# Attention heads scaled ahead of weight pieces, and the spread reciprocals read ahead of a weight load

## The chip, the cores and the metric

The kernel runs on one core of a Trainium2 chip. A core has a matrix engine (TensorE, written PE in the profile, with its weight loads as PEld), a vector engine (VectorE, DVE), an activation engine (ScalarE, ACT), a general engine (GpSimd, POOL), and a sync engine (SyncE, SP) that here issues nearly all transfers between the chip's main memory (HBM) and the on-chip memory. Sixteen DMA engines carry the transfers out. Each engine takes its instructions in the order in which they were written, and waits where an instruction needs what another engine or a transfer has not finished. The metric is the device time of one execution in microseconds (us); lower is better. The number given is the median of several runs.

## The reference

One decoder layer for 256 tokens of width 1024, all in float32: two token mixers side by side (attention with eight heads of 64, and a causal pooling over four window lengths), gated and added, then a feed-forward part with a short causal convolution. Cut to what matters here:

```python
h = rmsnorm(x, norm_mix_g)
q, k, v, u_pool, gate_logits = split(h @ w_in)
attn = moba_attention(rotary(rmsnorm(q)), rotary(rmsnorm(k)), v)  # SEQ = one block: causal softmax attention
pooled = multiscale_pool_mixer(u_pool, w_pool, pool_scale)
gates = sigmoid(gate_logits + b_gate)                              # (B, S, 2, D)
mixed = gates[:, :, 0] * (attn @ w_branch_attn) + gates[:, :, 1] * (pooled @ w_branch_pool)
x = x + mixed @ w_out
up = causal_depthwise_conv(rmsnorm(x, norm_ffn_g) @ w_up, conv_w, conv_b)
gate, val = split(up)
return x + (silu(gate) * val) @ w_down
```

The sequence of 256 is exactly one block of the block-sparse attention, so no earlier block can be chosen and plain causal attention remains.

## The kernel before

**Split operands.** Every large product is made of three matmuls on a shortened float32 type: with each operand split into a high part and the rest, it adds high x high, high x rest and rest x high (helper `mm3`, lines 103 to 105). For a weight tile of 128 x 2048 the high part is an ACT copy (`hi_...`, line 91) and the rest is a DVE subtraction (`lo_...`, line 95), each made in two pieces of 128 x 1024. Raw tiles go round in four buffers (`raw_...`). The list `order` gives the sequence of the weights: q, k, v, p (pooling input), g (gate logits), `bp` and `ba` (the two branch weights, two tiles each), `o` (four tiles), then `up` and `dn`. A piece is made wherever the program calls `ahead()`, which writes one high piece on ACT and one rest piece on DVE; when the last rest piece of a tile is written, `loads()` (line 135 issues) starts the load of the tile four places on. So the place of `ahead()` calls sets at which point in ACT's and DVE's queues the pieces stand, and through the buffers when SP can load.

**Stages.** Projections q, k, v; the pooling inputs; sixteen tiles of gate logits (`ps_g`), during which the scores and the softmax of the attention are done on DVE and ACT; then eight tiles of the pooling branch (`ps_bp`, loop over `j` from 0 to 7, called branch bp here), with the product of the softmax weights and the values (`values`, tile `ps_o`, line 625) written behind tile `j = 4` (`VALUES = 4`); then eight tiles of the attention branch (`ps_ba`), the output projection (`ps_out`), and the feed-forward part (`ps_up`, `ps_d`). Four PSUM banks go round among the tiles of the branches, so tile n+4 needs the bank that DVE has emptied of tile n.

**The attention's last steps.** The softmax weights are turned by 32 x 32 blocks on DVE and through HBM (`spill`, `fill`; transfers `home_w`, then `y<-home_w`). The sums of the exponentials are inverted, written to HBM (`home_sums`), and read back so that each reciprocal stands beside its values (tile `RS`, two reads, line 613, in `fill_late`). While the second half of the softmax is under way, loads are held back (`paused`), and `fill_late` writes one held load, `ba`'s second tile, ahead of the two reads of `RS`. `rounded` multiplies the values in PSUM by `RS` (DVE, line 644, four instructions of 128 x 256) and writes the high part of `heads` (ACT, line 91, four); `rests` writes the rest part of `heads` (DVE, line 95, four). `heads` is the moving operand of every matmul of `ps_ba`.

**Around them in the loop of bp.** Each `j` has on DVE the product of the finished bank with its gate (line 733) and, for `j` below 6, a product of one gate with the spread inverse norm `R1` (line 735); on ACT a sigmoid of one gate (line 656); and pieces of weights where `ahead()` is called. In the loop of `ps_ba`, DVE multiplies the bank by a gate (line 754), POOL adds the pooling branch (line 755), ACT writes the high part `mh` and DVE the rest `ml` for the output projection.

Of the kernel before, what the change touches and what calls it, by code (L numbers as in the profile page):

```python
# [10 lines left out]
ALU = mybir.AluOpType  # L11
# [3 lines left out]
S = 256  # L15
NT = S // P
D = 1024
KD = D // P
# [38 lines left out]
VALUES = 4  # L57
# [13 lines left out]
def hybrid_layer_kernel(ctx: ExitStack, tc: tile.TileContext, xq_d, xtok_d, par_d, wkv_d, wpg_d,  # L71
                        wpool_d, wba_d, wbp_d, wout_d, wup_d, wdn_d, out_d):
    nc = tc.nc
# [12 lines left out]
    def bank(name):  # L86
        return mm.tile([P, 512], F32, tag="mm", name=name)


    def high(hi, src, scale=1.0):  # L90
        nc.scalar.activation(hi, src, AF.Copy, scale=scale)  # L91

    def low(lo, hi, src, scale=None):
        if scale is None:
            nc.vector.tensor_tensor(lo, src, hi.bitcast(F32), ALU.subtract)  # L95
        else:
            nc.vector.scalar_tensor_tensor(lo, src, scale, hi.bitcast(F32), ALU.mult, ALU.subtract)
# [25 lines left out]
    def load(parts=1):  # L123
        c = loaded[0]
        if c == len(order):
            return
        loaded[0] += 1
        name, src = order[c]
        n = src.shape[-1]
        if c in cut_loads:  # L130
            parts = 2
        raws[c] = raw_p.tile([P, CH], F32, tag="raw", name=f"raw_{name}{c}")
        for i in range(parts):
            sl = slice(i * n // parts, (i + 1) * n // parts)
            nc.sync.dma_start(out=raws[c][:, sl], in_=src[:, sl])
# [53 lines left out]
    def loads(most=None):  # L189

        while loaded[0] - RAWBUFS in split and order[loaded[0] - RAWBUFS][0] != "q" and loaded[0] < len(order):
            if paused[0] if most is None else most == 0:
                break
            load()
            most = most if most is None else most - 1
# [3 lines left out]
    def ahead(upto=0):  # L199

        next_high()
        next_low()
        if at[1] - sum(p[0] < used[0] for p in pieces) < upto:
            next_high()
            next_low()

    def chunk(name):
        c = used[0]
        used[0] += 1
        spent.update(i for i in range(c) if order[i][0] != "dn")  # L210
        assert order[c][0] == name and all(p[0] != c or name == "dn" and p[3] for p in pieces[at[1]:]), (name, order[c][0])
        return his[c], los[c]
# [222 lines left out]
    def tick():  # L435
        clock[0] += 1
        for fn, args in due.pop(clock[0], []):
            fn(*args)


    def feature_tile(w, c, name):
        hi, lo = w
        ps = bank(f"ps_{name}")
        for k in range(KD):
            sl = slice(k * 256 + c * P, k * 256 + (c + 1) * P)
            mm3(ps[:, 0:S], (hi[:, sl], lo[:, sl]), (xhi[:, k, :], xlo[:, k, :]), k == 0, k == KD - 1)
        return ps
# [32 lines left out]
    for b in range(2):  # L480
        w = chunk("p")
        for c in range(2):
            ps = feature_tile(w, c, f"u{b}{c}")
# [35 lines left out]
    def gate(n):  # L519
        return gates[:, n // 2, n % 2, :]  # L520
# [63 lines left out]
    def turn_weights(hp, y, sm):  # L584
        turn(y, sm)
        home = spill(y, f"w{hp}")
        if hp < 2:
            later(1, fill_weights, hp, home, sm)
            return
        late.append((hp, home, sm))  # L590
        if hp == H // 2 - 1:
            nc.vector.reciprocal(rsum[:, 0:2 * H], rsum[:, 0:2 * H])
            yr = const.tile([P, 32], F32, name="yr")
            nc.vector.transpose(yr, rsum)
            far = spill(yr, "sums")
            loads(1)
            later(1, fill_late, far)
# [3 lines left out]
    def fill_weights(hp, home, sm):  # L601
        fill(home, sm)
        soft[hp] = sm.rearrange("p (a n r) -> p a n r", a=4, r=32)

    def fill_late(far):

        for weights in late:
            fill_weights(*weights)
        loads(1)
        RS.append(act.tile([P, H // 2 * NT * P], F32, tag="qk", name="RS"))  # L610
        for j in range(2):
            src = far.rearrange("(a i) r -> a (i r)", a=4)[None, :, j * S:(j + 1) * S].to_broadcast([DH, 4, S])
            nc.sync.dma_start(out=RS[0][j * DH:(j + 1) * DH, :].rearrange("p (a c) -> p a c", a=4), in_=src)
        paused[0] = False
        loads()

    def values(hps):

        po = ps2.tile([P, 2, 512], F32, tag="ps2", name=f"ps_o{hps[0]}")
        for i, hp in enumerate(hps):  # L620
            for b in range(2):
                for j in range(2):
                    h = 2 * hp + j
                    out = po[j * DH:(j + 1) * DH, i, 0:S].rearrange("p (a t r) -> p a t r", a=4, r=32)
                    nc.tensor.matmul(out[:, :, b:2, :], vn[:, b, h * DH:(h + 1) * DH],
                                     soft[hp][:, :, 3 * j + 2 * b:3 * j + b + 2, :], start=b == 0, stop=b == 1)
        return po

    def weighed(hp):
        return RS[0].rearrange("p (a h t r) -> p h a t r", a=4, t=NT, r=32)[:, hp]  # L630

    def natural(hp):
        return weighed(hp).rearrange("p a t r -> p t a r")

    def tokens(head, hp):
        return head[:, hp, :].rearrange("p (t a r) -> p t a r", t=NT, r=32)

    def rounded(hps, po):
        if not heads:
            both = act.tile([P, 2, KA, S], F32R, tag="at", name="heads")  # L640
            heads.extend(both[:, i] for i in range(2))
        for i, hp in enumerate(hps):
            v = weighed(hp)
            nc.vector.tensor_tensor(v, po[:, i, 0:S].rearrange("p (a t r) -> p a t r", a=4, r=32), v, ALU.mult)
            high(tokens(heads[0], hp), natural(hp))

    def rests(hps):
        for hp in hps:
            low(tokens(heads[1], hp), tokens(heads[0], hp), natural(hp))
# [3 lines left out]
    def sigmoids(n):  # L653
        for _ in range(min(n, len(waiting))):
            f = waiting.pop(0)
            nc.scalar.activation(gate(f), gate(f), AF.Sigmoid, bias=par[:, C_BG + f:C_BG + f + 1])
# [20 lines left out]
    for n in range(2 * KD):  # L677
# [16 lines left out]
        ps = feature_tile(w, c, f"g{n}")  # L694
# [18 lines left out]
    def branch(src, oph, opl, j, w):  # L713
        hi, lo = w
        ps = bank(f"ps_b{src}{j}")
        for k in range(4):
            sl = slice(k * 512 + (j % 4) * P, k * 512 + (j % 4 + 1) * P)
            mm3(ps[:, 0:S], (hi[:, sl], lo[:, sl]), (oph[:, k, :], opl[:, k, :]), k == 0, k == 3)
        return ps

    for j in range(KD):
        if j % 4 == 0:
            w = chunk("bp")
        ps = branch("p", poolh, pooll, j, w)
        if j == VALUES:
            pos = [(hps, values(hps)) for hps in ((0, 1), (2, 3))]
        if j % 2 == 1:
            tick()
            ahead()
        if j in (0, 2, 4, 6):  # L730
            ahead()
        sigmoids(1)
        nc.vector.tensor_tensor(gate(KD + j), ps[:, 0:S], gate(KD + j), ALU.mult)
        if j < len(plain):
            nc.vector.tensor_tensor(gate(plain[j]), gate(plain[j]), R1, ALU.mult)
        if j == VALUES:
            for po in pos:
                rounded(*po)
        if j == VALUES + 1:
            for hps, _ in pos:  # L740
                rests(hps)
    mixer.close()
    tmp = ctx.enter_context(tc.tile_pool(name="ffn", bufs=2))
    mh = act.tile([P, KD, S], F32R, tag="qk", name="mh")
# [2 lines left out]
    for j in range(KD):  # L747
        if j % 4 == 0:
            w = chunk("ba")
        ps = branch("a", heads[0], heads[1], j, w)  # L750
# [47 lines left out]
    for b in range(4):  # L798
        w = chunk("o")
        ps = [bank(f"ps_out{b}{c}") for c in range(2)]  # L800
# [74 lines left out]
    def up_tile(w, c, i):  # L875
        ps = bank(f"ps_up{i}_{c}")
        tile_part(w, (hhi, hlo), c, ps, range(KD))
        return ps
# [15 lines left out]
    ps = [bank("ps_up1_0")]  # L894
# [6 lines left out]
    for i in range(1, KF):  # L901
        if i > 1:
            w = chunk("up")
            ps = [up_tile(w, 0, i)]
# [101 lines left out]
```

## Time and profile before

| what | value |
|---|---|
| median of three runs | 328.73 us (328.5, 328.73, 332.89) |
| the profiled execution's own time | 328.95 us |
| its span, first to last instruction | 327.2 us |
| PE busy in it | 322.8 us, 99% |
| DVE busy | 259.4 us, 79% |
| ACT busy | 201.6 us, 62% |
| POOL busy | 71.8 us, 22% |
| moved by DMA | 69.72 MB, mean 213 GB/s |
| granted TensorE clock | 1.000 |

The profile is one execution, taken by the hardware profiler. A row of the timeline gives the start in us from the start of the span, the duration, the engine, the line of the program, the operation, its tile and operands, how many such instructions follow each other, and in brackets how long the engine stood idle just before it and what ended that. Matmuls are pipelined: a row of 0.28 us is followed by the next start after about 0.113 us, so the distance of starts, and not the duration, tells what one costs. A row of DMA issues gives the size and the time from issue to landing.

### The profile page before, as it was taken

The page shows a single profiled execution, that of the slowest core. Times are in us where ns is not written, and L with a number is a line of the kernel's source. Part 1 is how long each engine was busy: PE and PEld are TensorE (multiplying, and loading weights), DVE is VectorE, ACT ScalarE, POOL GpSimd, SP SyncE. Part 2 cuts the span into 40 slices and gives each one's busy share as a digit, 9 for nine tenths or more (in the row PEclk, how much of TensorE's full clock was granted, in tenths as well). Part 3 has the DMA queues.
Part 4 walks back from the last instruction along what each step waited for, and adds up shares of the span by engine and source line. Part 5 has one row for each costly group of instructions (what it writes and reads, how often), then busy time and mean ns, then how long its engine had stood idle before and what let it go on. Part 6 is the DMA issues. An engine that isn't in the chain of part 4 may idle for free.

```text
span 327.2 us, 6768 instructions
## 1 busy us (share of the span) xinstructions
PE 322.8 (99%) x2708; PEld 316.1 (97%) x2708; DVE 259.4 (79%) x447; ACT 201.6 (62%) x329; POOL 71.8 (22%) x89
## 2 busy tenths in 40 slices
PE   8999999999999999999999999999999999999995
PEld 8888899999999999999999999999999999999995
DVE  4939989989988966879997978686868686868834
ACT  5767519665995657669675647474747474746520
POOL 1007690000000151230421221212121212121330
PEclk9999999999999999999999999999999999999999
DMA  7999799837799833735527456464645454643003
GB/s 258 422 412 240 218 385 284 299 138 268 270 255 312 372 128 131 241 146 179 207 97 290 179 207 221 165 214 175 214 172 217 170 213 173 221 165 130 0 2 128
DMA packets 16542, 69.72 MB, mean 213 GB/s; under 512 B 2176, under 2 KB 7040, under 8 KB 9856
## 3 DMA queue, kind: packets, MB, share of 16 engines
q1 hardware_dynamic: 16096, 69.17, 59.5%
q8 instruction: 21, 0.34, 0.4%
q10 hardware_dynamic: 416, 0.13, 0.2%
q14 instruction: 9, 0.07, 0.1%
HBM read 65.61 MB, written 3.69 MB: 212 GB/s over the span
## 4 chain that ended last, share of the span: by engine, by line
PE 99%; DVE 0%; issue 0%
PE ps_up L104 12%; PE ps_up L103 12%; PE ps_up L105 12%; PE ps_d L867 6%; PE ps_d L866 6%; PE ps_d L868 6%; PE ps_g L103 5%; PE ps_g L104 4%; PE ps_g L105 4%; PE ps_q L333 4%; PE ps_k L333 3%; PE ps_v L333 3%; PE ps_out L104 2%; PE ps_out L105 2%; PE ps_out L103 2%; PE ps_warm L248 1%
## 5 line engine op out<-in xcount | busy, mean ns | idle before, releaser
L105 PE MATMUL ps_up<-hhi,lo_up 128*128 128x256 f32 x352 | 97.3, 276 | 0.0
L104 PE MATMUL ps_up<-hlo,hi_up 128*128 128x256 f32 x352 | 97.3, 276 | 0.0
L103 PE MATMUL ps_up<-hhi,hi_up 128*128 128x256 f32 x352 | 97.3, 276 | 0.0
L104 PEld LDWEIGHTS ps_up<-hlo,hi_up 128*128 128x128 f32 x352 | 66.1, 188 | 0.0
L103 PEld LDWEIGHTS ps_up<-hhi,hi_up 128*128 128x128 f32 x352 | 66.1, 188 | 0.0
L105 PEld LDWEIGHTS ps_up<-hhi,lo_up 128*128 128x128 f32 x352 | 66.1, 188 | 0.0
L95 DVE TENSOR_TENSOR lo_up<-raw_up,hi_up 128x1024 fp32r<-128x1024 f32 x44 | 54.7, 1262 | 7.3 <-ACT hi_up L91 7.3
L867 PE MATMUL ps_d<-al,hi_dn 128*128 128x256 f32 x176 | 48.6, 276 | 0.0
L868 PE MATMUL ps_d<-ah,lo_dn 128*128 128x256 f32 x176 | 48.6, 276 | 0.0
L866 PE MATMUL ps_d<-ah,hi_dn 128*128 128x256 f32 x176 | 48.6, 276 | 0.0
L91 ACT ACTIVATE hi_up<-raw_up 128x1024 fp32r<-128x1024 f32 x44 | 44.1, 1046 | 0.0
L848 POOL TENSOR_TENSOR c_v<-c_g,c_v 128x256 f32<-128x256 f32 x22 | 16.2, 737 | 121.4 <-DVE c_v L831 121.4
L91 ACT ACTIVATE ah<-c_v 128x256 fp32r<-128x256 f32 x22 | 9.2, 418 | 45.6 <-POOL c_v L848 45.6
L103 PE MATMUL ps_g<-xhi,hi_g 128*128 128x256 f32 x128 | 35.6, 278 | 0.0
L105 PE MATMUL ps_g<-xhi,lo_g 128*128 128x256 f32 x128 | 35.4, 277 | 0.0
L104 PE MATMUL ps_g<-xlo,hi_g 128*128 128x256 f32 x128 | 35.4, 277 | 0.0
L866 PEld LDWEIGHTS ps_d<-ah,hi_dn 128*128 128x128 f32 x176 | 33.1, 188 | 0.0
L867 PEld LDWEIGHTS ps_d<-al,hi_dn 128*128 128x128 f32 x176 | 33.1, 188 | 0.0
L868 PEld LDWEIGHTS ps_d<-ah,lo_dn 128*128 128x128 f32 x176 | 33.0, 188 | 0.0
L95 DVE TENSOR_TENSOR lo_dn<-raw_dn,hi_dn 128x1024 fp32r<-128x1024 f32 x22 | 27.8, 1263 | 0.4 <-ACT hi_dn L91 0.4
L836 DVE TENSOR_TENSOR u_v<-ps_up,R 128x256 f32<-128x256 f32 x22 | 9.3, 422 | 20.9 <-PE ps_up L105 20.8
L873 POOL TENSOR_TENSOR al<-c_v,ah 128x256 fp32r<-128x256 f32 x22 | 22.0, 1002 | 11.6 <-ACT ah L91 11.6
(196 smaller groups left out, 781.5 us busy)
## 6 DMA issues: line engine op xcount, KB each, us to landing
raw_up<-in_wup SPq DMA_DIRECT2D x22, 1024.0 KB, 4.8
raw_g<-in_wpg SPq DMA_DIRECT2D x8, 1024.0 KB, 7.3
raw_dn<-in_wdn SPq DMA_DIRECT2D x8, 1024.0 KB, 4.9
raw_o<-in_wout SPq DMA_DIRECT2D x4, 1024.0 KB, 10.1
raw_dn<-in_wdn SPq DMA_DIRECT2D x6, 512.0 KB, 4.8
raw_v<-in_wkv SPq DMA_DIRECT2D x2, 1024.0 KB, 15.3
raw_p<-in_wpg SPq DMA_DIRECT2D x2, 1024.0 KB, 12.8
raw_bp<-in_wbp SPq DMA_DIRECT2D x2, 1024.0 KB, 5.5
```

The lines of the kernel that those rows point to most:

```text
L91: nc.scalar.activation(hi, src, AF.Copy, scale=scale)
L95: nc.vector.tensor_tensor(lo, src, hi.bitcast(F32), ALU.subtract)
L103: nc.tensor.matmul(out, sh, mh, start=start, stop=False, **kw)
L104: nc.tensor.matmul(out, sh, ml, start=False, stop=False, **kw)
L105: nc.tensor.matmul(out, sl, mh, start=False, stop=stop, **kw)
L333: nc.tensor.matmul(pt[t][:, c:c + wide], sx[:, k, t * P:(t + 1) * P], wx[:, sl], start=k == 0 and c == 0 and sx is xhi and wx is hi, stop= ...
L836: nc.vector.tensor_tensor(u, ps[:, 0:S], R2, ALU.mult)
L848: nc.gpsimd.tensor_tensor(uc[1], g[1], uc[1], ALU.mult)
L866: nc.tensor.matmul(o, hi[:, sl], acch[i], start=first, stop=False, skip_group_check=True)
L867: nc.tensor.matmul(o, hi[:, sl], accl[i], start=False, stop=False, skip_group_check=True)
L868: nc.tensor.matmul(o, lo[:, sl], acch[i], start=False, stop=i == KF - 1, skip_group_check=True)
L873: nc.gpsimd.tensor_tensor(accl[i], act_i, acch[i].bitcast(F32), ALU.subtract)
```

## The change

Two things are moved; no instruction is added or taken away, and all operands and sizes stay.

```diff
@@ fill_late @@
         for weights in late:
             fill_weights(*weights)
-        loads(1)
         RS.append(act.tile([P, H // 2 * NT * P], F32, tag="qk", name="RS"))
@@ loop over j of the pooling branch @@
         if j == VALUES:
             pos = [(hps, values(hps)) for hps in ((0, 1), (2, 3))]
+        if j in (VALUES, VALUES + 1):
+            nc.vector.tensor_tensor(gate(KD + j), ps[:, 0:S], gate(KD + j), ALU.mult)
+            for hps, po in pos:
+                rounded(hps, po) if j == VALUES else rests(hps)
         if j % 2 == 1:
             tick()
             ahead()
         if j in (0, 2, 4, 6):
             ahead()
         sigmoids(1)
-        nc.vector.tensor_tensor(gate(KD + j), ps[:, 0:S], gate(KD + j), ALU.mult)
+        if j not in (VALUES, VALUES + 1):
+            nc.vector.tensor_tensor(gate(KD + j), ps[:, 0:S], gate(KD + j), ALU.mult)
         if j < len(plain):
             nc.vector.tensor_tensor(gate(plain[j]), gate(plain[j]), R1, ALU.mult)
-        if j == VALUES:
-            for po in pos:
-                rounded(*po)
-        if j == VALUES + 1:
-            for hps, _ in pos:
-                rests(hps)
     mixer.close()
```

The held load is not lost: the call of `loads()` at the end of `fill_late`, behind the reads of `RS`, writes it. In the rows below a trailing number tells buffers of one name apart.

On SP, from the load of `ba`'s first tile to the first loads of `o` (`raw_ba` and `raw_o` are weight loads, `y` the turned softmax weights, `RS` the reciprocals), before:

```order
L135 DMA raw_ba_1132<-in_wba 128x2048
L304 DMA y_814<-home_w_1120 32x4x192 x4
L304 DMA y_814<-home_w_1125 32x4x192 x4
L135 DMA raw_ba_1185<-in_wba 128x2048
L613 DMA RS<-home_sums 64x4x256 x2
L135 DMA raw_o_1230<-in_wout 128x2048
```

and now:

```order
L135 DMA raw_ba_1132<-in_wba 128x2048
L304 DMA y_814<-home_w_1120 32x4x192 x4
L304 DMA y_814<-home_w_1125 32x4x192 x4
L612 DMA RS<-home_sums 64x4x256 x2
L135 DMA raw_ba_1188<-in_wba 128x2048
L135 DMA raw_o_1230<-in_wout 128x2048
```

The two reads of `RS` have moved ahead of the load of `ba`'s second tile.

On DVE, from the first rest piece of `ba`'s second tile to the emptying of bp's tile `j = 6` (rows of `xq<-ps_bp` empty a bank, rows of `xq<-xq,R` are the products with `R1`), before:

```order
L95 TENSOR_TENSOR lo_ba_1331<-raw_ba_1185,hi_ba_1330 128x1024
L733 TENSOR_TENSOR xq<-ps_bp_1373,xq 128x256
L735 TENSOR_TENSOR xq<-xq,R_169 128x256
L644 TENSOR_TENSOR RS<-ps_o_1386,RS 128x4x64 x2
L644 TENSOR_TENSOR RS<-ps_o_1395,RS 128x4x64 x2
L95 TENSOR_TENSOR lo_o_1405<-raw_o_1230,hi_o_1404 128x1024
L733 TENSOR_TENSOR xq<-ps_bp_1422,xq 128x256
L735 TENSOR_TENSOR xq<-xq,R_169 128x256
L95 TENSOR_TENSOR heads<-RS,heads 128x256 x4
L733 TENSOR_TENSOR xq<-ps_bp_1444,xq 128x256
```

and now:

```order
L727 TENSOR_TENSOR xq<-ps_bp_1373,xq 128x256
L643 TENSOR_TENSOR RS<-ps_o_1386,RS 128x4x64 x2
L643 TENSOR_TENSOR RS<-ps_o_1395,RS 128x4x64 x2
L95 TENSOR_TENSOR lo_ba_1331<-raw_ba_1188,hi_ba_1330 128x1024
L739 TENSOR_TENSOR xq<-xq,R_169 128x256
L727 TENSOR_TENSOR xq<-ps_bp_1422,xq 128x256
L95 TENSOR_TENSOR heads<-RS,heads 128x256 x4
L95 TENSOR_TENSOR lo_o_1415<-raw_o_1230,hi_o_1414 128x1024
L739 TENSOR_TENSOR xq<-xq,R_169 128x256
L737 TENSOR_TENSOR xq<-ps_bp_1444,xq 128x256
```

The second rest piece of `ba`'s second tile now stands behind the scaling of the values instead of ahead of it; the first rest piece of `o` stands behind the rest parts of `heads` and thereby still ahead of the emptying of `j = 6`, as the product with `R1` does.

On ACT, at the same place (`xq<-xq,par` is a sigmoid), before:

```order
L656 ACTIVATE xq<-xq,par 128x256 x2
L91 ACTIVATE hi_o_1404<-raw_o_1230 128x1024
L656 ACTIVATE xq<-xq,par 128x256
L91 ACTIVATE heads<-RS 128x256 x4
L91 ACTIVATE hi_o_1404<-raw_o_1230 128x1024
```

and now:

```order
L655 ACTIVATE xq<-xq,par 128x256 x2
L91 ACTIVATE heads<-RS 128x256 x4
L91 ACTIVATE hi_o_1414<-raw_o_1230 128x1024
L655 ACTIVATE xq<-xq,par 128x256
L91 ACTIVATE hi_o_1414<-raw_o_1230 128x1024
```

The high parts of `heads` have moved ahead of the first high piece of `o` and of one sigmoid. PE's and POOL's sequences are the same as before.

## The prediction

> **What bounds the kernel now.** I read the page's busy times first, then who PE waited for, then PE's rows at the place of the change, and last the queues of SP, ACT and DVE there.
>
> The first lines are from the page (busy time, and the chain that ended last by engine), the next three from the lists of waits of PE and of its weight loads (in total, times, longest, in us), and the last two the first projection's row and the end of the chain:
>
> ```profile
> PE 322.8 (99%) x2708; PEld 316.1 (97%) x2708; DVE 259.4 (79%) x447; ACT 201.6 (62%) x329; POOL 71.8 (22%) x89
> PE 99%; DVE 0%; issue 0%
> ...
> PE ps_warm L248 <- DVE ones L216: 1.1, 1, 1.1
> ...
> PEld ps_warm L248 <- DVE ones L216: 1.0, 1, 1.0
> PEld ps_bp L103 <- DVE xq L735: 0.2, 1, 0.2
> ...
> 5.05 1.20 PE L333 MATMUL ps_q<-hi_q,xhi 128*128 128x256 f32 x4
> ...
> 323.77 0.13 PE ps_d L868
> 323.92 0.42 DVE xq L930
> ```
>
> PE works without a pause from 5.05 us to the last product at 323.9. Its only wait is 1.1 us for the first constant, far ahead of the change, and its weight loads show one of 0.2 us in branch bp. The chain is PE for 99%. So what DVE, ACT and SP do sooner is worth nothing unless PE waits for it, and the rows leave at most 0.2 us of such waiting. The change can only lose, or do nothing.
>
> At the place of the change PE's rows read:
>
> ```profile
> 104.09 0.28 PE L105 MATMUL ps_bp<-poolh,lo_bp 128*128 128x256 f32 x1
> 104.30 1.52 PE L625 MATMUL ps_o<-sm,vn 128*64 128x256 f32 x16
> 105.65 1.47 PE L625 MATMUL ps_o<-y,vn 128*64 128x256 f32 x16
> 107.05 0.39 PE L103 MATMUL ps_bp<-poolh,hi_bp 128*128 128x256 f32 x1
> 107.28 0.28 PE L104 MATMUL ps_bp<-pooll,hi_bp 128*128 128x256 f32 x1
> ...
> 111.25 0.28 PE L103 MATMUL ps_ba<-heads,hi_ba 128*128 128x256 f32 x1
> 111.36 0.28 PE L104 MATMUL ps_ba<-heads,hi_ba 128*128 128x256 f32 x1
> ...
> 113.97 0.28 PE L103 MATMUL ps_ba<-heads,hi_ba 128*128 128x256 f32 x1
> ```
>
> The 0.2 us lies at 107.05 to 107.28, where PE returns from the values' other kind of product. The steps that count are two: 111.36, where the first product with a rest part of `heads` starts, and 113.97, where the third tile of `ps_ba` needs the bank that DVE has emptied of bp's `j = 6`. How much room had DVE there?
>
> DVE's rows in order of time:
>
> ```profile
> 102.68 1.23 DVE L95 TENSOR_TENSOR lo_ba<-raw_ba,hi_ba 128x1024 fp32r<-128x1024 f32 x1 [1.04 <-ACT hi_ba L91]
> 103.82 0.42 DVE L733 TENSOR_TENSOR xq<-ps_bp,xq 128x256 f32<-128x256 f32 x1
> 104.15 0.42 DVE L735 TENSOR_TENSOR xq<-xq,R 128x256 f32<-128x256 f32 x1
> ...
> 105.15 1.22 DVE L95 TENSOR_TENSOR lo_ba<-raw_ba,hi_ba 128x1024 fp32r<-128x1024 f32 x1
> ...
> 106.95 1.42 DVE L644 TENSOR_TENSOR RS<-ps_o,RS 128x256 f32<-128x256 f32 x4
> 108.56 1.23 DVE L95 TENSOR_TENSOR lo_o<-raw_o,hi_o 128x1024 fp32r<-128x1024 f32 x1 [0.20 <-ACT hi_o L91]
> ...
> 110.37 1.43 DVE L95 TENSOR_TENSOR heads<-RS,heads 128x256 fp32r<-128x256 f32 x4
> 111.71 0.75 DVE L733 TENSOR_TENSOR xq<-ps_bp,xq 128x256 f32<-128x256 f32 x2
> ```
>
> The starts give the step of each kind: a rest piece 1.14 us (102.68 to 103.82), a small product 0.33 (103.82 to 104.15), four of them 1.34 (110.37 to 111.71). The first rest part of `heads` is ready at 110.37 + 0.42 = 110.79, 0.57 ahead of PE; the following ones keep pace, since PE takes three products of 0.113 for each. Bank `j = 6` is free at 111.71 + 0.42 = 112.13, 1.84 ahead. DVE reached this point after waiting at 102.68 for `hi_ba`, the first high piece of `ba`'s second tile, and that for its load. That load is what the change moves back.
>
> **The change on SP.** The rows of SP's queue, then size and time from issue to landing of these transfers (KB, us), then ACT's rows:
>
> ```profile
> 90.80 5.18 SPq L304 DMA_DIRECT2D y<-home_w  x8
> 96.11 0.36 SPq L135 DMA_DIRECT2D raw_ba<-in_wba  x1
> 96.62 1.45 SPq L613 DMA_DIRECT2D RS<-home_sums  x2
> 98.17 8.55 SPq L135 DMA_DIRECT2D raw_o<-in_wout  x4
> ...
> y<-home_w SPq DMA_DIRECT2D x1, 96.0 KB, 3.0
> raw_ba<-in_wba SPq DMA_DIRECT2D x1, 1024.0 KB, 5.4
> RS<-home_sums SPq DMA_DIRECT2D x2, 256.0 KB, 7.5
> ...
> 101.58 1.06 ACT L91 ACTIVATE hi_ba<-raw_ba 128x1024 fp32r<-128x1024 f32 x1 [2.21 <-DMA raw_ba<-in_wba]
> ...
> 107.47 1.06 ACT L91 ACTIVATE hi_o<-raw_o 128x1024 fp32r<-128x1024 f32 x1 [2.68 <-DMA raw_o<-in_wout]
> 108.83 1.33 ACT L91 ACTIVATE heads<-RS 128x256 fp32r<-128x256 f32 x4
> ```
>
> Landings follow the issues: the last read of `y`, issued shortly ahead of 96, lands near 99; `ba` at 96.11 + 5.4 = 101.5, where ACT starts; the reads of `RS` at about 104.4 (second issue 97.3 by half of 1.45, and some 7.2 on); the first `o` at 107.47. The distances are 2.5, 2.9 and 3.1 us. It looks like one line in which each waits for the one ahead.
>
> Now the reads of `RS` go first, at 96.0, and `ba` is issued 1.35 to 1.45 us later, near 97.5. The line is then still busy with `y` until 99, so no transfer time is lost in between. If it is one line, `RS` and `ba` together end when they ended before, and `ba`, now second, lands at 104.4 and not 101.5: a delay D of 2.9 us. Bounds from the same rows: if transfers share the engines and none holds up the other, D is the issue alone, 1.35; if the whole 2.9 of `RS` comes on top of the later issue, D is 4.3. I take 2.9, since the row of ACT and the row of landings agree on the line. `RS` itself lands near 102, well ahead of its use.
>
> [...]
>
> **The change on DVE, with that delay.** The first rest piece starts at 102.68 + D. Behind it come, in the new order: this piece and four small products, 2.47 (as 102.68 to 105.15 before); bp's `j = 4`, 0.33; the four of `RS`, 1.34; the second rest piece, 1.14; the product with `R1` and bp's `j = 5`, 0.67. The rest parts of `heads` start at 108.63 + D, the first is ready at 109.05 + D. PE needs it at 111.36, so PE stands still if D exceeds 2.3; at 2.9 it waits 0.6 us. The values themselves (PE done at 107.05) are no limit then. Next, four rest parts 1.34, the first rest piece of `o` 1.14, and one product 0.33: bank `j = 6` is emptied from 111.44 + D and free at 111.86 + D, needed at 113.97. That limit is D = 2.1, so at 2.9 it makes the stall 0.8 in all. With D = 1.35 nothing stalls, with 4.3 it is 2.2 us.
>
> **The other moves, at nothing.** With D = 0 the new order alone would have the rest parts of `heads` ready up to 1.5 us sooner, worth nothing, since PE was not waiting. On ACT the high parts of `heads` no longer stand behind `hi_o`, which waited 2.68 for its load; they follow DVE's products by a step and are done before the rest parts begin. The price is that `hi_o` starts near 110 and not 107.47, and the rest pieces of the first `o` end some 3 us later; that tile's first use is the output projection, at 111.25 + 96 products of 0.113 = 122.1. The second rest piece of `ba` ends near 111 against its use in the fifth tile of `ps_ba`, 111.25 + 48 x 0.113 = 116.7. The loads that these pieces let start (the last `o`, the first `up`) go 3 to 5 us later into a stage with the DMA engines half idle:
>
> ```profile
> 111.20:122.00 10.80, 10.80 (x97) 10.80 (x97) 8.04 (x18) 5.79 (x12) 5.30 (x6) 1.00 0.52 190
> ...
> 113.31 2.35 POOL L755 TENSOR_TENSOR xq<-xq 128x256 f32<-128x256 f32 x2 [63.48 <-DVE xq L754]
> ...
> 124.89 0.42 DVE L95 TENSOR_TENSOR ml<-xq,mh 128x256 fp32r<-128x256 f32 x1 [1.08 <-ACT mh L91]
> ```
>
> (The window's row gives busy time of PE, PEld, DVE, ACT, POOL, then clock, DMA share 0.52, GB/s.) DVE has 2.8 us of idle time there to catch up; POOL has nothing to do until 113.31. The last rest part `ml` is done at 125.3, and the output projection takes it after 42 products, at 122.1 + 4.8 = 126.9. That leaves 1.6 us, so what DVE lags behind PE is absorbed, and everything after it moves by PE's stall.
>
> **The sum.** The profiled execution took 328.95 us, its span being 327.2; it would take 328.95 + 0.8 = 329.75. It lies 0.22 above the median of the runs, so I forecast 328.73 + 0.8 = 329.5.
>
> **Rivals.** *No stall*: the load lands by 103.6 (D below 2.1), because transfers share engines or because `RS` without a weight load ahead goes faster. For it speaks that the reads carry only 512 KB; against it the landings in line. The time is 328.5 to 328.8, the lower end with the 0.2 us of PEld gone. *A longer stall*: D of 3.7 to 4.3 or a little more, if the small reads hold up the load by their whole time; stall 1.6 to 2.2, time 330.3 to 330.9. *Slower by over 2%*: the reads, now first, hold up SP's queue and all weights behind them. It decides from a stall of 6.6 us, that is D of 8.7, with `ba` landing at 110.2. Against it: in the row at 96.62 the reads were issued 0.15 us after the load's issue ended, so what they wait for was there by then, and standing first they can lose at most 0.6 us on SP. Time from 335.3.
>
> [...]
>
> **How the numbers follow.** Stall near 0.8 (0.3 to 1.5): 0.47. No stall: 0.30. Longer stall: 0.20. Slower by over 2%: 0.02. Faster by over 2%, 6.6 us, has no place in PE's rows: 0.01. Two per cent is about what a measurement of this kernel can tell from no change. Faster 0.01, same 0.97, slower 0.02. The range takes in the first rival and most of the longer stall, with some room for a run like the third of before (332.89): 328.3 to 331.2.
>
> **What would show it.** In the changed profile `hi_ba` for `ba`'s second tile starts near 104.5, DVE idles some 4 us ahead of that rest piece, and PE shows a wait at the first tile of `ps_ba` for `heads` and one at the third for line 737, 0.8 us together. The forecast is wrong if `ba` lands by 103.6 (no wait), if `RS` lands later than 104, or if PE waits anywhere behind `ps_ba`.

## The result

| | before | changed |
|---|---|---|
| median, 22 runs each | 328.75 us (328.27 to 333.34) | 331.23 us (329.83 to 334.21) |
| ratio to before | | 1.0063, 95% interval 1.0038 to 1.0089 |
| profiled execution, its span | 327.2 us | 329.1 us |

The ratio leaves disturbed runs out; applied to 328.75 it gives 330.8 us, 2.1 us more than before, with 1.2 to 2.9 for the interval. The two medians lie 2.5 us apart. By the bound of 2% that is no change, but it is a loss clear of noise. The profiled execution took 330.91 us; what the runs of 333 us and more lost beyond it is not shown.

The page of the changed kernel (busy times, chain by engine):

```profile
PE 323.7 (98%) x2708; PEld 316.3 (96%) x2708; DVE 259.2 (79%) x447; ACT 201.6 (61%) x329; POOL 71.5 (22%) x89
PE 93%; DVE 4%; POOL 1%; issue 1%; ACT 0%; POOLq 0%
```

From its list of what PE's weight loads waited for (in total, times, longest):

```profile
PEld ps_ba L104 <- DVE heads L95: 1.1, 1, 1.1
...
PEld ps_out L104 <- DVE ml L95: 0.6, 2, 0.3
```

The chain is no longer PE alone. PE now waits for the rest part of `heads`, and in the output projection for `ml`. SP's queue at the place of the change:

```profile
90.68 5.32 SPq L304 DMA_DIRECT2D y<-home_w  x8
96.11 1.32 SPq L612 DMA_DIRECT2D RS<-home_sums  x2
97.52 0.55 SPq L135 DMA_DIRECT2D raw_ba<-in_wba  x1
```

The issues there, with size and median time to landing:

```profile
raw_ba<-in_wba SPq DMA_DIRECT2D x1, 1024.0 KB, 6.9
RS<-home_sums SPq DMA_DIRECT2D x2, 256.0 KB, 4.9
```

Rows from the timeline of ACT, then of DVE (`...` marks rows left out, here and below):

```profile
104.54 1.06 ACT L91 ACTIVATE hi_ba<-raw_ba 128x1024 fp32r<-128x1024 f32 x1 [5.14 <-DMA raw_ba<-in_wba]
...
105.63 1.23 DVE L95 TENSOR_TENSOR lo_ba<-raw_ba,hi_ba 128x1024 fp32r<-128x1024 f32 x1 [4.37 <-ACT hi_ba L91]
...
111.57 1.42 DVE L95 TENSOR_TENSOR heads<-RS,heads 128x256 fp32r<-128x256 f32 x4
...
114.38 0.74 DVE L737 TENSOR_TENSOR xq<-ps_bp,xq 128x256 f32<-128x256 f32 x2
115.04 0.41 DVE L752 TENSOR_TENSOR xq<-ps_ba,xq 128x256 f32<-128x256 f32 x1
```

The load that was moved back is issued 1.4 us later than before but lands at 97.52 + 6.9 = 104.4, 2.9 later. DVE stands idle for 4.37 us, and its queue hands the delay on: the rest parts of `heads` start at 111.57 and not at 110.37. The row at 114.38 empties the banks of `j = 6` and `j = 7`, the row at 115.04 the first bank of `ps_ba`. PE's timeline, at the first and third tile of `ps_ba` and in `ps_out`:

```profile
110.87 0.28 PE L103 MATMUL ps_ba<-heads,hi_ba 128*128 128x256 f32 x1
112.03 0.39 PE L104 MATMUL ps_ba<-heads,hi_ba 128*128 128x256 f32 x1 [0.89 <-DVE heads L95]
112.26 0.28 PE L105 MATMUL ps_ba<-heads,lo_ba 128*128 128x256 f32 x1
...
114.66 0.28 PE L105 MATMUL ps_ba<-heads,lo_ba 128*128 128x256 f32 x1
114.84 0.38 PE L103 MATMUL ps_ba<-heads,hi_ba 128*128 128x256 f32 x1
115.06 0.28 PE L104 MATMUL ps_ba<-heads,hi_ba 128*128 128x256 f32 x1
...
124.71 0.28 PE L105 MATMUL ps_out<-mh,lo_o 128*128 128x256 f32 x1
124.89 0.38 PE L103 MATMUL ps_out<-mh,hi_o 128*128 128x256 f32 x1
125.42 0.39 PE L104 MATMUL ps_out<-ml,hi_o 128*128 128x256 f32 x1
125.64 0.28 PE L105 MATMUL ps_out<-mh,lo_o 128*128 128x256 f32 x1
125.76 0.28 PE L103 MATMUL ps_out<-mh,hi_o 128*128 128x256 f32 x1
126.08 0.39 PE L104 MATMUL ps_out<-ml,hi_o 128*128 128x256 f32 x1
```

and DVE's for the two `ml` that these rows at 125.42 and 126.08 wait for (the sixth and the seventh of eight, ready at 124.87 + 0.49 and 125.62 + 0.41):

```profile
124.87 0.49 DVE L95 TENSOR_TENSOR ml<-xq,mh 128x256 fp32r<-128x256 f32 x1 [0.75 <-ACT mh L91]
...
125.62 0.41 DVE L95 TENSOR_TENSOR ml<-xq,mh 128x256 fp32r<-128x256 f32 x1
```

Distances of starts beyond the usual 0.113 are PE's losses, also where the list of waits names none. At the first tile 1.16 and 0.23 stand for two such steps: 1.16 us lost. At the third tile 0.18 and 0.22: 0.18 lost. In `ps_out`, 0.18 ahead of 124.89, then 0.53, 0.22 and 0.32, and 0.23 behind the last row: 0.9 lost. Together 2.25; PE had come to the first of them 0.38 us earlier than in the profile of before (110.87 against 111.25), and the span is 1.9 longer.

### The profile page after: what moved, and what is told of

It is laid out like the page before. It is cut to its first block, busy times and chain, and to the rows that moved or that the text cites. A ratio compares the mean times of both kernels' runs of the same rounds, so it can differ in the third digit from the quotient of the medians.

```text
span 329.1 us, 6770 instructions
## 1 busy us (share of the span) xinstructions
PE 323.7 (98%) x2708; PEld 316.3 (96%) x2708; DVE 259.2 (79%) x447; ACT 201.6 (61%) x329; POOL 71.5 (22%) x89
## 4 chain that ended last, share of the span: by engine, by line
PE 93%; DVE 4%; POOL 1%; issue 1%; ACT 0%; POOLq 0%
PE ps_up L105 12%; PE ps_up L103 12%; PE ps_up L104 12%; PE ps_d L866 6%; PE ps_d L864 6%; PE ps_d L865 6%; PE ps_g L103 5%; PE ps_g L105 4%; PE ps_g L104 4%; PE ps_q L333 3%; PE ps_k L333 3%; PE ps_v L333 3%; PE ps_out L104 2%; PE ps_out L105 2%; PE ps_out L103 2%; PE ps_warm L248 1%
```

## The experiments

Two theories were set against each other. Theory L: the load of `ba`'s second tile lands later, and DVE's queue passes that on to PE. Theory O: the new order on DVE and ACT makes the loss by itself.

**The reads of `RS` first, and nothing else** (the kernel before, with one line out):

```diff
             fill_weights(*weights)
-        loads(1)
         RS.append(act.tile(...))
```

> Only the reads of RS ahead of the load of ba's second tile; DVE and ACT in the order of before. Theory L (the load lands some 3 us later, and DVE's queue passes that on to PE): hi_ba of that tile starts near 104.5; in the old order the first rest part of heads is ready near 113.5, so PE waits 2.1 to 2.5 us at the first tile of ps_ba, all in one place, and nowhere in ps_out, since PE is then as late as DVE; time 330.9 to 331.4. Theory O (the new order on DVE and ACT makes the loss, because pieces of o end later): no wait of PE, 328.75 as before.

Measured: 333.62 us in the median, ratio 1.0100 (1.0060 to 1.0139). In its profile the load lands near 105.2, and PE waits for `heads` as L says, 0.4 us for the high part and 2.3 for the rest. ACT's row for the load, then the list of PE's waits:

```profile
105.22 1.06 ACT L91 ACTIVATE hi_ba<-raw_ba 128x1024 fp32r<-128x1024 f32 x1 [5.85 <-DMA raw_ba<-in_wba]
```

```profile
PE ps_ba L104 <- DVE heads L95: 2.3, 1, 2.3
...
PE ps_ba L103 <- ACT heads L91: 0.4, 1, 0.4
```

Three windows of it (busy time of PE, PEld, DVE, ACT, POOL, then granted clock, DMA share, GB/s):

```profile
111.50:114.20 2.70, 0.41 (x2) 0.21 (x2) 2.70 (x7) 2.70 (x7) 0.00 (x0) 0.99 0.86 346
114.20:117.40 3.20, 3.20 (x15) 3.20 (x16) 2.06 (x7) 0.78 (x2) 0.00 (x0) 0.50 0.05 15
117.40:120.40 3.00, 3.00 (x27) 3.00 (x27) 2.34 (x4) 1.28 (x3) 2.39 (x2) 0.98 0.26 49
```

Behind the wait the clock is granted at 0.50 for 3.2 us, in which PE starts 15 products where 3.2 / 0.113 = 28 would fit; that costs 13 x 0.113 = 1.5 us more, which neither theory had reckoned with. Theory O, which expected 328.75, has fallen. The time expected of L, 330.9 to 331.4, was too low by this and by a landing 0.7 us later than reckoned.

**The new order alone** (the changed kernel, with the line put back):

```diff
             fill_weights(*weights)
+        loads(1)
         RS.append(act.tile(...))
```

> Only the new order on DVE and ACT; the load of ba's second tile stays ahead of the reads of RS. Theory L: the load lands near 101.5 as before, the rest parts of heads are ready by 109.5, PE waits nowhere; time 328.6 to 328.9. Theory O: PE waits for ml in ps_out and the time is 0.8 to 2 us above before, 329.5 to 330.8.

Measured: 328.66 us, ratio 0.9960 (0.9924 to 0.9995). PE waits for nothing behind the start; its weight loads show the 0.2 us of before at `ps_bp`, here and in the other versions without a loss. Its timeline has ACT's row for the load, and DVE's for the rest parts of `heads`:

```profile
101.01 1.06 ACT L91 ACTIVATE hi_ba<-raw_ba 128x1024 fp32r<-128x1024 f32 x1 [2.42 <-DMA raw_ba<-in_wba]
...
109.32 1.42 DVE L95 TENSOR_TENSOR heads<-RS,heads 128x256 fp32r<-128x256 f32 x4
```

The rest parts start 1.05 us sooner than before, of which 0.57 is the load, read by ACT at 101.01 and not at 101.58, and the rest the order. That gives room and no time. The ratio below 1 was tried again with the same kernel:

> The same kernel as order_alone, on another chip or at another time, to see whether its ratio of 0.996 to before holds. If the new order makes the kernel faster, the ratio lies below 1 again with its interval; if it only leaves PE as it was, the interval takes in 1 and the median stays at 328.5 to 329.

Measured: 328.74 us, ratio 0.9994 (0.9983 to 1.0006). So the order leaves the time as it was; the first ratio is not confirmed.

**The load in two halves** (the changed kernel; `ba_second` is the second tile of `ba`):

```diff
-        if c in cut_loads:
+        if c in cut_loads or c == ba_second:
             parts = 2
```

> The changed kernel with the load of ba's second tile issued as two halves. If transfers go in one line, the first half lands 1.2 us earlier, near 103.3, and the first piece on ACT starts then: no wait for heads at ps_ba, DVE about 1 us late in ps_ba, PE waits about 0.6 us for ml in ps_out; time 329.2 to 329.6. If the halves share the engines and land together: as the changed kernel, 330.8 to 331.3.

Measured: 331.05 us, ratio 1.0038 (1.0005 to 1.0072), the time that was expected if nothing were gained. The issues in two short windows, with size and time to landing (the first half and the second read of `RS`, then the second half), and ACT's row:

```profile
raw_ba<-in_wba SPq DMA_DIRECT2D x1, 512.0 KB, 6.8
RS<-home_sums SPq DMA_DIRECT2D x1, 256.0 KB, 5.8
...
raw_ba<-in_wba SPq DMA_DIRECT2D x1, 512.0 KB, 7.5
```

```profile
104.58 1.06 ACT L91 ACTIVATE hi_ba<-raw_ba 128x1024 fp32r<-128x1024 f32 x1 [5.04 <-DMA raw_ba<-in_wba]
```

The halves land one behind the other, at 97.7 + 6.8 = 104.5 and, issued half a microsecond later, near 105.7; so here they went in line, 1.2 us apart. But the first was not sooner than the whole tile in the changed kernel, the second read of `RS` ending near 102.8 here and 102.1 there. One execution can't say which part of that is the halving. The run leaves open what halves are worth.

**The load ahead of the reads of `y`** (the changed kernel):

```diff
     def fill_late(far):
+        loads(1)
         for weights in late:
             fill_weights(*weights)
```

> The changed kernel with the load of ba's second tile issued ahead of the eight reads of y, and so ahead of those of RS too. Theory L: the load lands by 100, y and RS land 2.4 us later than in the changed kernel (RS near 104.5), still ahead of their use (values at 104, RS product at 106); PE waits nowhere; time 328.6 to 328.9. Theory O: as the changed kernel, 330.8 to 331.3. If y comes too late for the values, PE waits at ps_o.

Measured: 328.57 us, ratio 0.9976 (0.9950 to 1.0003). PE waits nowhere. With the same reads of `RS` ahead of the loads of `o`, the loss of the changed kernel is gone, so the place of this one load in the line decides. Run again beside its counterpart in the old order:

> The same kernel as load_before_y, beside the one with the old order, to tell which of the two runs more evenly: 328.4 to 328.8 in the median, highest run below 329.5.

Measured: 328.87 us, ratio 0.9987 (0.9965 to 1.0008); the median lies 0.07 above what was expected. The twelve runs lie between 328.41 and 329.34.

> The kernel before with the load of ba's second tile ahead of the eight reads of y; DVE and ACT in the order of before. Theory L: ba lands by 98, DVE never waits for its pieces, PE waits nowhere, 328.4 to 328.8; the rest parts of heads still stand behind the first piece of o, so a late load of o can cost something in single runs. If the new order is what keeps PE from waiting: above 329 in a good part of the runs, as before on this chip.

Measured (the same line put into the kernel before): 329.49 us, ratio 1.0016 (0.9989 to 1.0043), twelve runs from 328.41 to 335.37; the expected 328.4 to 328.8 was missed. Its timeline shows where the old order is tight, on ACT and then on DVE:

```profile
108.09 1.06 ACT L91 ACTIVATE hi_o<-raw_o 128x1024 fp32r<-128x1024 f32 x1 [5.87 <-DMA raw_o<-in_wout]
...
109.45 1.32 ACT L91 ACTIVATE heads<-RS 128x256 fp32r<-128x256 f32 x4
...
109.18 1.22 DVE L95 TENSOR_TENSOR lo_o<-raw_o,hi_o 128x1024 fp32r<-128x1024 f32 x1 [1.21 <-ACT hi_o L91]
...
110.99 1.42 DVE L95 TENSOR_TENSOR heads<-RS,heads 128x256 fp32r<-128x256 f32 x4
```

`heads` stands behind the first piece of `o` on both engines, and that waits for its own load. The rest part is ready at 111.41, just when PE, which came to the tile at 111.30, asks for it with its second product 0.11 later. By these rows a later landing of `o` would be paid in full. That this is what the higher single runs paid is argued; no profile of one was taken. No version was faster than before in a way that held: the one ratio wholly below 1, of the first run of the new order alone, was not confirmed.

**Each read of `RS` twice** (the changed kernel; the second copy goes into a tile `again` that nothing reads):

```diff
             nc.sync.dma_start(out=RS[0][j * DH:(j + 1) * DH, :].rearrange(...), in_=src)
+            nc.sync.dma_start(out=again[j * DH:(j + 1) * DH, :].rearrange(...), in_=src)
```

> The changed kernel with each read of RS issued twice, the second time into a buffer that nothing uses, all four ahead of the load of ba's second tile. If transfers go in one line, ba lands some 3 us later than in the changed kernel, 107.0 to 108.0, and PE waits 3.6 to 4.8 us at the first tile of ps_ba; with the granted clock at half for some 3 us behind a wait of that length, as the run with the reads first alone showed, the time is 334 to 336. If the extra reads share the engines with the load: as the changed kernel or up to 1 us above, 331 to 332.

Measured: 334.71 us in four runs, ratio 1.0169 (1.0134 to 1.0205). The time is as expected of one line, its parts are not: the load landed at 98.59 + 9.9 = 108.5 for an expected 107.0 to 108.0, and PE's wait was shorter and elsewhere. The issue with its time to landing, and ACT's row:

```profile
raw_ba<-in_wba SPq DMA_DIRECT2D x1, 1024.0 KB, 9.9
```

```profile
108.56 1.06 ACT L91 ACTIVATE hi_ba<-raw_ba 128x1024 fp32r<-128x1024 f32 x1 [9.58 <-DMA raw_ba<-in_wba]
```

PE's wait, and a window that takes in its end, with the granted clock (0.66) ahead of the last two numbers (lines stand two further on in this kernel, so line 739 is here the emptying of a bank):

```profile
PE ps_bp L103 <- DVE xq L739: 2.6, 1, 2.6
```

```profile
110.50:115.50 5.00, 4.24 (x23) 4.24 (x24) 5.00 (x13) 3.85 (x9) 0.00 (x0) 0.66 0.64 264
```

Another 512 KB of such reads delayed the load by another 4.0 us (108.56 against 104.54), of which 1.1 is the later issue. PE stood already at bp's tile `j = 6`, since DVE, idle for 8.04 us ahead of the rest piece, had not emptied `j = 2` (done at 110.79 + 0.42 = 111.21, PE went on at 111.26). Again the clock dropped behind the wait, to 0.66 in the mean of this window.

**One piece of `o` later** (the changed kernel):

```diff
-        if j in (1, 3):
+        if j == 1:
             ahead()
...
     low(ml[:, KD - 1, :], mh[:, KD - 1, :], gate(KD - 1))
     ahead()
+    ahead()
```

> The changed kernel with one piece of o (its high piece on ACT and rest piece on DVE, written behind the fourth tile of ps_ba) written behind the last ml instead. Theory M (the waits of PE for ml in ps_out come from DVE standing 2.2 us later than before through all of ps_ba while PE stands only 1 us later): ml is ready 1.1 us sooner, PE's waits in ps_out of 0.8 us vanish, the wait for heads at the first tile of ps_ba stays near 1 us; time 0.8 us below the changed kernel, 329.8 to 330.5. Rival: ml is late because of ACT's and POOL's steps ahead of it, not of that piece: 330.8 to 331.3 as the changed kernel. If the pieces of o's second tile then come too late, PE waits behind the first two tiles of ps_out.

Measured: 330.25 us, ratio 1.0020 (0.9994 to 1.0046). PE's waits in `ps_out` are gone, that for `heads` is 0.3 us, as its list of waits and DVE's row of the seventh `ml` show:

```profile
PE ps_ba L104 <- DVE heads L95: 0.3, 1, 0.3
```

```profile
123.71 0.41 DVE L95 TENSOR_TENSOR ml<-xq,mh 128x256 fp32r<-128x256 f32 x1
```

In this execution the load landed 0.8 us sooner than in the changed kernel's, so not all of the gain is the piece's. But the seventh `ml` is ready at 124.12, while PE asks for it near 124.5 (124.28 before, less 0.55 because PE came sooner, plus some 0.75 lost in `ps_ba`). With the piece still ahead of it, 1.14 us of DVE, it would have come 0.8 too late. So the rows bear theory M out. The times agree with it, but do not show the gain by themselves: the ratio's interval overlaps that of the changed kernel (1.0038 to 1.0089).

## Why the prediction was right and where it was wrong

**The direction and the first link were right.** No PE wait was there to remove, so nothing was to be gained: the order alone left the time where it was. The load fell behind the reads of `RS`, as forecast from the order of landings: it landed at 104.4, as forecast. DVE's rows followed from the delay of 2.95 us as worked out, to the hundredth for `heads` (108.63 + 2.95 = 111.58; 111.57 measured). The waits came where they were announced, for `heads` at the first tile and for the bank of `j = 6` at the third.

That the landing was hit to the tenth is luck. The forecast took the end of the second read of `RS` before as 104.4, with some 7.2 us from issue to landing. That is the time of the first read; the second took longer, as a short window of the profile of before has it:

```profile
RS<-home_sums SPq DMA_DIRECT2D x1, 256.0 KB, 7.7
```

Issued at 97.3, it landed near 105.0. By the forecast's own rule, that `RS` and `ba` together end when they ended before, the delay would have been 3.5 us and the stall 1.4. In the changed kernel the two ended 0.6 sooner than that. Nor is the landing the same in every execution: behind the reads of `RS` the whole tile landed 6.9 us after its issue in the changed kernel, 7.6 with the reads first alone and 8.1 with one piece of `o` later.

**The size was wrong: 0.8 us forecast, 2.1 by the ratio, 1.9 in the profile.** By the prediction's own signs it failed at one point, "if PE waits anywhere behind `ps_ba`": PE waits in `ps_out`. The range to 331.2 takes in the 330.8 by the ratio, with the median of 331.23 at its edge, but it reached that far for the longer stall, which is not what happened. Three terms:

- *The step that failed* is "DVE has 2.8 us of idle time there to catch up ... what DVE lags behind PE is absorbed". It hardly catches up. Most of DVE's pauses in `ps_ba` are the way round from DVE over POOL and ACT back to DVE, and they are as long in the changed kernel as before: 0.75, 0.83, 0.74 and 0.75 us ahead of the first, second, fourth and sixth `ml` in both. The first `ml` in the changed kernel's timeline:

```profile
117.67 0.50 DVE L95 TENSOR_TENSOR ml<-xq,mh 128x256 fp32r<-128x256 f32 x1 [0.75 <-ACT mh L91]
```

  and in that of before the emptying of the first bank of `ps_ba`, then the first, the sixth and the seventh `ml`, with PE's rows that use the last two:

```profile
112.81 0.42 DVE L754 TENSOR_TENSOR xq<-ps_ba,xq 128x256 f32<-128x256 f32 x1 [0.34 <-PE ps_ba L105]
...
115.45 0.49 DVE L95 TENSOR_TENSOR ml<-xq,mh 128x256 fp32r<-128x256 f32 x1 [0.75 <-ACT mh L91]
...
122.65 0.49 DVE L95 TENSOR_TENSOR ml<-xq,mh 128x256 fp32r<-128x256 f32 x1 [0.75 <-ACT mh L91]
...
123.41 0.41 DVE L95 TENSOR_TENSOR ml<-xq,mh 128x256 fp32r<-128x256 f32 x1
...
123.94 0.28 PE L104 MATMUL ps_out<-ml,hi_o 128*128 128x256 f32 x1
...
124.28 0.28 PE L104 MATMUL ps_out<-ml,hi_o 128*128 128x256 f32 x1
```

  DVE empties `j = 6` 2.67 us late (114.38 against 111.71) and the first bank of `ps_ba` 2.23 (115.04 against 112.81): of the 2.8 us of idle time it used the 0.34 in which it had waited for PE, and little else. From there on nothing is made up: the first `ml` is 2.22 us late, and so are the sixth and the seventh (123.41 before, 125.62 now). The forecast looked at the room of the last `ml` alone, 1.6 us. The sixth had 0.80 (ready at 123.14, used at 123.94) and the seventh 0.46 (ready at 123.82, used at 124.28). PE being 1 us late and DVE 2.2, that room was gone. Price: 0.9 us for a forecast of nothing.
- The first wait took 1.16 us for a forecast of 0.6. Of the difference 0.38 is where PE stood: the load landed at 104.4, as forecast, but PE reached the tile 0.38 us earlier in this execution than in the one the sum was made from (110.87 against 111.25). Some 0.1 is the first step behind a wait, 0.23 us instead of 0.113.
- The third tile cost 0.18 for a forecast of 0.2.

**The rivals.** *No stall* needed the load by 103.6 and fell: it landed at 104.4, and in all five profiles in which it stood behind the reads of `RS` it landed behind them (in the changed kernel 2.3 us behind, 104.4 against 102.1). *A longer stall* gave the time that came, 330.3 to 330.9, but by a delay of 3.7 to 4.3; the delay was 2.95, and the loss came downstream. *Slower by over 2%* did not come. The reads alone, without the new order, lose 1.0%, and twice the reads 1.7%; in the profiles of both a lower granted clock adds to the wait (0.50 for 3.2 us with the reads alone, 0.66 over a window of 5.0 us with the reads twice), a price that no sum of the forecast has.

So the two parts of the change work against each other. The reads ahead of the load cost time, and the new order seems to take part of that back (1.0063 against 1.0100 for the reads alone, with intervals that overlap; in the profiles a span of 329.1 against 331.7), by putting `heads` ahead of pieces that nobody waits for yet.

## What to carry to other kernels

Before a small read with little to gain goes ahead of a large load, read from the landings what it costs the load: here 2.9 us, of which the later issue is 1.4. Then look at who stands behind the load, in the queue of the engine that needs it. Where an engine is late, count its lag through to the last place that uses its results, result by result: the pauses that were a round trip through other engines, 0.74 to 0.83 us each, were no reserve here. And where PE is the bound and never waits, ask of each reordering only what room it takes or gives.

## What the runs showed of the hardware

In the profiles of two runs PE's wait cost more than itself. Behind 0.4 + 2.3 us of waiting with one product in between, with the reads first alone, the granted clock was 0.50 for 3.2 us. Behind a single wait of 2.6 us, with the reads twice, PE's starts first lay 0.11 to 0.12 us apart for about 0.7 us, behind a first step of 0.22, and then 0.21 apart for another 3.3. After the changed kernel's wait of 0.9 us the clock stayed at 1.00. Behind the start no profile has a wait of PE between 0.9 and 2.3 us, so where the drop sets in is not shown.

The reads of `RS` carry little and take long: the two, 256 KB each, landed 4.9 us after issue in the median in the changed kernel; 1 MB of weights at the same place in the line took 5.4 before. From landing to landing in the changed kernel, the two reads took 3.5 us behind the last read of `y` (98.6 to 102.1), and the 1 MB behind them 2.3 (to 104.4). While they began, between 97 and 98 us, the DMA engines' busy share was 0.37 in the changed kernel and 0.78 before, where the weights went first. The window of the changed kernel (DMA share and GB/s are the last two):

```profile
97.00:98.00 1.00, 1.00 (x11) 1.00 (x10) 0.77 (x2) 1.00 (x4) 0.00 (x0) 1.00 0.37 116
```

and of before:

```profile
97.00:98.00 1.00, 1.00 (x12) 1.00 (x11) 0.39 (x2) 1.00 (x4) 0.00 (x0) 1.00 0.78 234
```

What limits such reads was not tried.
